# Attention with keys on partitions: row maxima ahead, probabilities stationary in the value product

## The chip, the cores and the metric

The kernel runs on one core of one Trainium2 chip. TensorE (PE in the profile; PEld is its weight load) multiplies matrices and accumulates in PSUM. It holds one operand, the weights or stationary side, loaded by an instruction of its own; the other operand, the moving side, then streams through it column by column. VectorE (DVE), ScalarE (ACT) and GpSimd (POOL) work on SBUF and PSUM, and SyncE (SP) issues transfers. Each engine has an instruction queue of its own that runs in order; semaphores hold an instruction until what it reads has been written. The metric is the device time of one execution in microseconds (us), the median over the runs.

## The reference

A sequence of 2048 tokens of width 1024 passes through a Mamba-2 layer, then through a latent attention layer with 16 heads, each with a residual addition; a last RMSNorm ends it. The change touches the attention of the second layer. A query and a key of a head have 96 entries (64 without and 32 with a rotary position), a value has 64.

```python
s = jnp.einsum('bqhd,bkhd->bhqk', q_nope[:, q0:kv_len], k_nope[:, :kv_len]) + \
    jnp.einsum('bqhr,bkr->bhqk', q_rope[:, q0:kv_len], k_rope[:, :kv_len])
s = s.astype(jnp.float32) * scale
mask = (q0 + local)[:, None] >= jnp.arange(kv_len)[None, :]
p = jax.nn.softmax(jnp.where(mask, s, -jnp.inf), axis=-1).astype(v.dtype)
outs.append(jnp.einsum('bhqk,bkhd->bqhd', p, v[:, :kv_len]))
...
o = o.reshape(Bsz, S, MLA_HEADS * V_HEAD) * jax.nn.silu(gate)
return o @ w_out
```

All of it is in fp32. The kernel keeps that precision with pairs of fp16 numbers, a high half and a low half (what the high one leaves); a product of two pairs is three matmuls, high by high, high by low and low by high.

## The kernel before

The program runs its stages one after the other on one core: the Mamba-2 layer, the projections of the attention layer, the attention itself (`attention`, `heads`), and `back`, which multiplies by the gate, projects, adds the residual and normalizes. The projections write K, V and Q as fp16 pairs to memory in the device (`kn_d`, `kr_d`, `v_d`, `qn_d`, `q1_d`, `q2_d`), and the attention loads them from there.

`heads` works through 64 jobs, 16 heads by 4 blocks of 512 queries. A job has units, one for each tile of 128 keys that its queries can see: 4, 8, 12 and 16 for the four blocks, 640 in all. The last four units of a job lie on the diagonal and are used for 512, 384, 256 and 128 queries.

The work of a job goes in two orders that are woven together:

- `scores` takes the four tiles of 128 queries (`j`) one by one. `cuts` divides the visible keys into chunks of at most 512. For each chunk `mm3` (L86 to L90) makes three matmuls with the queries stationary and the keys moving, into a PSUM bank "mm" (L1232; at the start also "tr"); the last chunk gets the causal mask by a further matmul (L1234). VectorE takes each chunk's row maximum (L1239) and, over the chunks, the negated one, `nm` (L1242, or L1237 where there is one chunk). ScalarE then takes the exponential with `nm` as bias and sums each row as it goes (L1247), a chunk at a time; the fp32 result `Pr` has queries on its partitions.
- `turn` makes the keys stand on partitions, unit by unit: up to four fp32 transposes on TensorE into a bank "tr" (L1272), a copy by ScalarE with a factor of 32768 for the high half of `PTs` (L1275), and the low half by VectorE, which reads the same bank (L1278).
- `values` multiplies, with the 128 columns of V (64 high, 64 low) stationary and the probabilities moving: one matmul for each half (L1292, L1293), accumulated over a job's units in another bank "tr".
- `finish` copies the outcome (L1299). SP stores 64 of its rows (L1301), and GpSimd's queue adds the other 64 to them in memory (L1305). The sums' reciprocals go to `ri_d` once a head (L1308 to L1317); `back` loads them, spreads each over 64 partitions and multiplies the gate by them (L1387, L1388).

The order of TensorE's instructions is the program's own (`manual_schedule`); the other engines' queues are set by a scheduler that follows it. The table `CREDIT` says, for each block, query tile and chunk, which turns ("T") and value products ("V") follow a chunk's scores; the first 20 chunks (`LAG`) have none behind them, and a value product comes at least two units (`DEPTH`) after its turn. So scores of one job stand among turns and products of the job before.

K, V and Q are loaded through GpSimd's queue (L1162 to L1176): K into a pool of two buffers, V and Q into "xT" buffers of which there are eight. Those of head h + 1 are ordered while head h is computed, K and V at its third block. SP's queue carries the stores, the weights and the loads of `back`.

Of the kernel before, what the change touches and what calls it, by code (L numbers as in the profile page):

```python
# [21 lines left out]
P = 128  # L22
# [5 lines left out]
NH = 16  # L28
# [9 lines left out]
NP = 24  # L38
# [3 lines left out]
LAG = 20  # L42
DEPTH = 2
CREDIT = (
    (("VT",), ("TV",), ("VT",), ("TV",)),
    (("", "VTVT"), ("", "TTVV"), ("", "TTVV"), ("", "TTVV")),
    (("TT", "", "VVTV"), ("TV", "", "VTTV"), ("TV", "", "TTVV"), ("TTV", "", "TVV")),
    (("T", "", "", "VVTTVTV"), ("T", "V", "", "VTTVTV"), ("T", "V", "V", "TVTTV"), ("TV", "V", "", "TVTVT")),
)
MAGIC = 12582912.0  # L50
PSCALE = 32768.0
# [20 lines left out]
class Net:  # L72
# [1019 lines left out]
    def mla_up(self, b, tables):  # L1092
# [24 lines left out]
        while ahead:  # L1117
            (n, w), ahead = ahead, next(todo, None)
            qT = self.qT
            for i in range(2 if n == 6 else 4):  # L1120
# [3 lines left out]
                elif n < 4:  # L1124
# [5 lines left out]
                    self.pair16(uv[:, :, 0, :], uv[:, :, 1, :], ps.rearrange("p (h d) -> p h d", h=8), 2.0 ** -15)  # L1130
# [10 lines left out]
    def open_heads(self):  # L1141

        self.tail = ExitStack()
        self.hp = self.tail.enter_context(
            self.tc.tile_pool(name="hp", bufs=2, side="right", reuse_waits="tile"))
        self.keys, self.vals, self.quer = {}, {}, {}
        self.load_k(0, 0, NB - 1)

    def load_vq(self):

        self.load_k(0, NB - 1, NB)
        self.load_q(0, 0)
        self.load_v(0)
        for n in range(1, NB):
            self.load_q(0, n)

    def load_k(self, h, lo, hi):

        nc, ts = self.nc, slice(lo * TB, hi * TB)
        if lo == 0:  # L1160
            self.keys[h] = self.t(self.hp, "K", [96, 2, T], F16, bufs=2)
        nc.gpsimd.dma_start(self.keys[h][0:64, :, ts], self.kn_d[h * 64:(h + 1) * 64, :, ts])  # L1162
        nc.gpsimd.dma_start(self.keys[h][64:96, :, ts], self.kr_d[:, :, ts])

    def load_v(self, h):

        V = self.vals[h] = self.t(self.xq, "xT", [P, T // P, P], F16, bufs=8)
        self.nc.gpsimd.dma_start(V, self.v_d[:, h * P:(h + 1) * P].rearrange("(k p) d -> p k d", p=P))

    def load_q(self, h, n):  # L1170

        nc, ts = self.nc, slice(n * TB, (n + 1) * TB)
        Q = self.quer[h, n] = self.t(self.xq, "xT", [96, 2, TB], F16, bufs=8)
        nc.gpsimd.dma_start(Q[0:64], self.qn_d[h * 64:(h + 1) * 64, :, ts])
        nc.gpsimd.dma_start(Q[64:80], self.q1_d[h * 16:(h + 1) * 16, :, ts])
        nc.gpsimd.dma_start(Q[80:96], self.q2_d[h * 16:(h + 1) * 16, :, ts])  # L1176
# [15 lines left out]
    def heads(self, sp):  # L1192
        nc, v = self.nc, self.nc.vector
        begun = []
        keys, vals, quer = self.keys, self.vals, self.quer

# [11 lines left out]
        def scores(h, qb, st):  # L1208

            if h + 1 < NH:  # L1210
                if qb == 2:
                    self.load_k(h + 1, 0, NB)
                    self.load_v(h + 1)
                self.load_q(h + 1, qb)
            Q, K = quer.pop((h, qb)), keys[h]
            late, total = [], sums[h][:, 4 * qb:4 * qb + 4]
            sm = self.t(sp, "sm", [P, 4, 4], bufs=2) if qb else total.unsqueeze(2)
            for j in range(4):
                qs = slice(j * P, (j + 1) * P)
                parts = cuts(qb * TB + (j + 1) * P)  # L1220
                nb = len(parts)
                mx, nm = (self.t(sp, m, [P, n], bufs=4) for m, n in (("mx", 4), ("nm", 1)))
                p = {}
                st["P"].append(p)
                banks = []
                for n, (c0, w) in enumerate(parts):
                    if late:
                        late.pop(0)()
                    begun.append(0)
                    s = self.t(self.pp, "tr" if len(begun) <= 18 and len(begun) % 2 == 1 else "mm", [P, TB], bufs=4)  # L1230
                    ks = slice(c0, c0 + w)
                    self.mm3(s[:, :w], Q[:, 0, qs], Q[:, 1, qs], K[:, 0, ks], K[:, 1, ks], True, n < nb - 1)  # L1232
                    if n == nb - 1:
                        nc.tensor.matmul(s[:, w - P:w], self.idb, self.mk, start=False, stop=True)  # L1234
                    banks.append((s, w))
                    if nb == 1:
                        v.tensor_reduce(nm, s[:, :w], AX.X, ALU.max, negate=True)  # L1237
                    else:
                        v.tensor_reduce(mx[:, n:n + 1], s[:, :w], AX.X, ALU.max)  # L1239
                    if n == nb - 1:  # L1240
                        if nb > 1:
                            self.last_max = v.tensor_reduce(nm, mx[:, :nb], AX.X, ALU.max, negate=True)  # L1242

                        def exp(n, j=j, nb=nb, parts=parts, banks=banks, nm=nm, p=p):
                            s, w = banks[n]
                            x = self.t(sp, "Pr", [P, TB], bufs=NP)
                            nc.scalar.activation(x[:, :w], s[:, :w], AF.Exp, bias=nm, accum_out=sm[:, j, n:n + 1])  # L1247
                            for c in range(0, w, P):
                                p[(parts[n][0] + c) // P] = x[:, c:c + P]
                            if j == 3 and n == nb - 1 and nb > 1:  # L1250
                                behind.append(lambda: v.tensor_reduce(total, sm[:, :, :nb], AX.X, ALU.add))
                                if nb != 3:
                                    behind.pop(0)()

                        late += [lambda n=n, f=exp: f(n) for n in range(nb)]
                        if nb > 2:
                            late.pop(0)()
                        if nb > 3 and j == 0:
                            with self.tc.issue_after(self.last_max.ins):
                                while behind:  # L1260
                                    behind.pop(0)()
                    self.place = qb, j, n, nb
                    yield CREDIT[qb][j][n]
            for f in late:
                f()

        def turn(h, qb, kb, st):

            jj = max(kb - 4 * qb, 0)
            pt = self.t(self.pp, "tr", [P, TB], bufs=4)  # L1270
            for j in range(jj, 4):
                nc.tensor.transpose(pt[:, j * P:(j + 1) * P], st["P"][j][kb], self.ident)  # L1272
            c = slice(jj * P, TB)
            u = self.t(sp, "PTs", [P, 2, TB], F16, bufs=5)
            nc.scalar.activation(u[:, 0, c], pt[:, c], AF.Copy, scale=PSCALE)  # L1275

            def low():
                v.scalar_tensor_tensor(u[:, 1, c], pt[:, c], PSCALE, u[:, 0, c], ALU.mult, ALU.subtract)  # L1278
# [269 lines left out]
```

## Time and profile before

| | |
|---|---|
| three runs | 3070.26, 3069.26, 3067.33 us; median 3069.26 us |
| profiled execution, its span | 3068.0 us |
| attention, from about 1998.5 to 2880.2 us | 881.7 us |
| behind it, `back` | 187.8 us |
| chain that ended last, by engine | PE 66%, DVE 16%, ACT 8%, issue 4%, DMA 4% |
| transfers in all | 457.10 MB, 149 GB/s in the mean |

The profile records one execution. A row of it gives a line of the kernel, the engine, the operation, the output and inputs by the program's names, and the shape; busy times are sums of records, which on TensorE overlap, since matmuls are pipelined. From the start of one matmul to the start of the next is what one takes of the array. "Idle before" is the time that an engine stood still ahead of a group's instructions, and behind it stands what ended it. "mm" and "tr" are PSUM banks, four each; "Pr" holds the exponentials, "PTs" the turned halves, "xT" is a buffer for several kinds of operand (V and Q here). A view of windows gives each engine's busy time and the granted clock of TensorE in a stretch.

### The profile page before, as it was taken

The page shows a single profiled execution, that of the slowest core. Times are in us where ns is not written, and L with a number is a line of the kernel's source. Part 1 is how long each engine was busy: PE and PEld are TensorE (multiplying, and loading weights), DVE is VectorE, ACT ScalarE, POOL GpSimd, SP SyncE. Part 2 cuts the span into 40 slices and gives each one's busy share as a digit, 9 for nine tenths or more (in the row PEclk, how much of TensorE's full clock was granted, in tenths as well). Part 3 has the DMA queues.
Part 4 walks back from the last instruction along what each step waited for, and adds up shares of the span by engine and source line. Part 5 has one row for each costly group of instructions (what it writes and reads, how often), then busy time and mean ns, then how long its engine had stood idle before and what let it go on. Part 6 is the DMA issues. An engine that isn't in the chain of part 4 may idle for free.

```text
span 3068.0 us, 51041 instructions
## 1 busy us (share of the span) xinstructions
PE 2988.2 (97%) x17758; PEld 1762.9 (57%) x17758; DVE 2309.3 (75%) x5034; ACT 1930.8 (63%) x4920; POOL 616.0 (20%) x842
## 2 busy tenths in 40 slices
PE   7899999999999999999999999999999999999998
PEld 3456655555555555545555455466666666666787
DVE  6789888778777787887755544488888888888576
ACT  8777656665666665565534333388888888888522
POOL 0212122211222122222111211322222222222100
PEclk9999999999999999999999999999999999999999
DMA  8665435454455466354466555622323223232484
GB/s 286 229 227 189 152 104 195 162 167 154 163 193 167 136 199 224 125 196 145 150 208 203 184 186 165 191 71 56 68 54 66 53 55 65 54 88 76 131 268 154
DMA packets 205065, 457.10 MB, mean 149 GB/s; under 512 B 28115, under 2 KB 57555, under 8 KB 203365
## 3 DMA queue, kind: packets, MB, share of 16 engines
q1 hardware_dynamic: 176948, 375.94, 38.0%
q0 software_dynamic: 27856, 77.89, 10.0%
q8 instruction: 140, 2.29, 0.3%
q14 instruction: 121, 0.98, 0.1%
HBM read 340.99 MB, written 112.73 MB: 148 GB/s over the span
## 4 chain that ended last, share of the span: by engine, by line
PE 66%; DVE 16%; ACT 8%; issue 4%; DMA 4%; SPq 1%; POOL 1%; ACTq 0%; DVEq 0%; POOLq 0%
PE mm L88 14%; PE mm L89 13%; PE mm L90 13%; PE tr L1272 6%; PE tr L89 4%; DVE cacc L616 4%; PE tr L88 4%; PE tr L90 3%; PE tr L1292 3%; PE tr L1293 3%; ACT Pr L1247 2%; PE tr L883 1%; ACT PTs L1275 1%; DMA big<-cumT 1%; DVE mx L1239 1%
## 5 line engine op out<-in xcount | busy, mean ns | idle before, releaser
L1278 DVE SCALAR_TENSOR_TENSOR PTs<-tr,PTs 128x512 f16<-128x512 f32 (+3 forms) x640 | 375.3, 607 | 103.0 <-ACT PTs L1275 95.1
L1247 ACT ACTIVATE Pr<-mm,nm 128x512 f32<-128x512 f32 (+2 forms) x631 | 398.0, 639 | 13.7 <-DVE nm L1242 13.5
L1275 ACT ACTIVATE PTs<-tr 128x512 f16<-128x512 f32 (+3 forms) x640 | 330.2, 542 | 119.9 <-PE tr L1272 111.0
L1239 DVE TENSOR_REDUCE mx<-mm 128x1 f32<-128x512 f32 (+2 forms) x569 | 335.1, 616 | 18.1 <-PE mm L90 15.2
L1272 PE MATMUL tr<-pack,Pr 128*128 128x128 f32 x2176 | 320.9, 273 | 6.5 <-DVE PTs L1278 2.4
L88 PE MATMUL mm<-xT,wsp 128*128 128x512 f16 x800 | 306.0, 383 | 7.1 <-ACT wsp L119 3.9
L89 PE MATMUL mm<-xT,wsp 128*128 128x512 f16 x800 | 305.2, 382 | 0.0
L90 PE MATMUL mm<-xT,wsp 128*128 128x512 f16 x800 | 304.7, 381 | 0.0
L1272 PEld LDWEIGHTS tr<-pack,Pr 128*128 128x128 f32 x2176 | 252.9, 141 | 80.1 <-ACT Os L1299 7.9
L88 PE MATMUL mm<-wsp,xT 128*128 128x512 f16 (+1 forms) x640 | 230.8, 362 | 4.8 <-ACT craw L610 4.7
L89 PE MATMUL mm<-wsp,xT 128*128 128x512 f16 (+1 forms) x640 | 231.9, 363 | 3.2 <-DVE wsp L120 3.2
L616 DVE SCALAR_TENSOR_TENSOR cacc<-craw,pack,cacc 128x512 f32<-128x512 f32 x288 | 215.6, 777 | 23.5 <-ACT cacc L614 22.5
L90 PE MATMUL mm<-wsp,xT 128*128 128x512 f16 (+1 forms) x640 | 231.9, 363 | 0.0
L88 PE MATMUL mm<-K,xT 96*128 96x512 f16 (+2 forms) x639 | 222.5, 348 | 5.3 <-ACT Pr L1247 3.3
L90 PE MATMUL mm<-K,xT 96*128 96x512 f16 (+2 forms) x639 | 221.8, 347 | 0.0
L1292 PE MATMUL tr<-PTs,xT 128*128 128x512 f16 (+3 forms) x640 | 221.0, 347 | 0.4 <-DVE PTs L1278 0.3
L89 PE MATMUL mm<-K,xT 96*128 96x512 f16 (+2 forms) x639 | 221.2, 346 | 0.0
L1293 PE MATMUL tr<-PTs,xT 128*128 128x512 f16 (+3 forms) x640 | 219.2, 347 | 0.0
L89 PEld LDWEIGHTS <-xT 128*128 128x128 f16 (+1 forms) x1408 | 137.9, 98 | 141.2 <-issue 30.9
L90 PEld LDWEIGHTS <-xT 128*128 128x128 f16 (+1 forms) x1408 | 136.8, 97 | 132.6 <-issue 4.8
L88 PEld LDWEIGHTS <-xT 128*128 128x128 f16 (+1 forms) x1408 | 137.4, 98 | 117.7 <-issue 4.7
L88 PE MATMUL mm<-wsp,yT 128*128 128x512 f16 (+1 forms) x512 | 197.5, 386 | 2.4 <-DVE sz L640 2.1
(458 smaller groups left out, 6801.3 us busy)
## 6 DMA issues: line engine op xcount, KB each, us to landing
wsp<-wi_d SPq DMA_DIRECT2D x96, 512.0 KB, 3.8
big<-cumT SPq DMA_DIRECT2D x64, 512.0 KB, 4.4
wraw<-in_ssm_w_out_dram SPq DMA_DIRECT2D x96, 256.0 KB, 3.6
wi_d<-wsp SPq DMA_DIRECT2D x32, 512.0 KB, 3.6
wsp<-wo_d SPq DMA_DIRECT2D x32, 512.0 KB, 3.5
wsp<-wu_d SPq DMA_DIRECT2D x28, 512.0 KB, 3.7
hx<-in_ssm_w_in_dram SPq DMA_DIRECT2D x48, 256.0 KB, 4.1
wraw<-in_ssm_w_in_dram SPq DMA_DIRECT2D x48, 256.0 KB, 3.9
```

Of the source, the lines that this page charges most:

```text
L88: mm(out, l_hi, r_hi, start=start, stop=False)
L89: mm(out, l_hi, r_lo, start=False, stop=False)
L90: mm(out, l_lo, r_hi, start=False, stop=stop)
L616: nc.vector.scalar_tensor_tensor(acc, raw[:, k:k + TB], wk[k], acc, ALU.mult, ALU.add)
L883: nc.tensor.matmul(yi[t, hc], E[:, h, t], Xd[:, hc], start=True, stop=True)
L1239: v.tensor_reduce(mx[:, n:n + 1], s[:, :w], AX.X, ALU.max)
L1247: nc.scalar.activation(x[:, :w], s[:, :w], AF.Exp, bias=nm, accum_out=sm[:, j, n:n + 1])
L1272: nc.tensor.transpose(pt[:, j * P:(j + 1) * P], st["P"][j][kb], self.ident)
L1275: nc.scalar.activation(u[:, 0, c], pt[:, c], AF.Copy, scale=PSCALE)
L1278: v.scalar_tensor_tensor(u[:, 1, c], pt[:, c], PSCALE, u[:, 0, c], ALU.mult, ALU.subtract)
L1292: nc.tensor.matmul(st["O"][:, c], vals[h][:, kb, :], u[:, 0], start=kb == 0, stop=False)
L1293: nc.tensor.matmul(st["O"][:, c], vals[h][:, kb, :], u[:, 1], start=False, stop=kb == nk - 1)
```

## The change

The maximum, the scores and the value product are each laid out anew, and the order table is replaced by rules.

**Maxima.** `maxima` makes only the high-by-high matmul of a chunk (L1235), masks the last chunk of a query tile (L1237), and takes the row maximum (L1238). At the end of a job the four maxima of each row become -max/64 + ln(16)/64, split into two fp16 halves in `turned` (L1243 to L1250). The maximum from the high halves need not be exact: the same number is taken out above and below the quotient. `row` turns these with one matmul (L1255), casts (L1257), stores them to `m_d` and loads them back (L1258, L1259, both on SP) into rows 96 and 97 of Q's high half, one query a column. Rows 96 and 97 of K's high half hold 64.0, so the subtraction becomes part of the score matmul.

**Scores.** A unit now has its keys stationary and up to 512 queries moving, so that the scores stand with keys on partitions at once (L1269 to L1271, three passes, the first with 98 rows). A diagonal unit gets the mask (L1273). ScalarE takes the exponential without bias or sums (L1275) into `x`, copies it from there as the high half (L1277), and the low half is `x` less the high half (L1279), on GpSimd for 128 of the units off the diagonal (two in five, by number) and on VectorE for 512.

**Value product.** The probabilities are stationary, for each 128 queries, and V moves: 130 columns for the high half (low V, high V, and two columns of 2^-14, by which the row sums come out), 66 for the low one (high V and those columns). `finish` adds the two parts, divides by the sum (L1306 to L1313), and `store` turns the outcome of two heads at once with four fp32 transposes (L1323), copies it (L1325) and stores 128 rows (L1327).

**Order.** At each unit come the maxima that are due (`due`: those of a job 7 units ahead, spread so that mostly one falls on a step), then rows or stores whose step has come (rows 2 steps after their last maximum, stores 4 steps after), then this unit's scores, then the value product of the unit 3 steps back (`HELD`). Ahead of the first unit stand 17 chunks of maxima.

**Loads and buffers.** K and V of a head lie in one of two fixed tiles, `K0` and `K1`. All loads of K, V and Q are on SP's queue: Q of a job when the maxima of the job two before it begin, K and V of head h + 2 behind the last value product of head h. `ri_d` and its loads and multiplication in `back` are gone.

```diff
@@ -1127,7 +1123,7 @@
-                    self.pair16(uv[:, :, 0, :], uv[:, :, 1, :], ps.rearrange("p (h d) -> p h d", h=8), 2.0 ** -15)
+                    self.pair16(uv[:, :, 1, :], uv[:, :, 0, :], ps.rearrange("p (h d) -> p h d", h=8), 2.0 ** -15)
...
-        nc.gpsimd.dma_start(Q[0:64], self.qn_d[h * 64:(h + 1) * 64, :, ts])
...
+        nc.sync.dma_start(Q[0:64], self.qn_d[h * 64:(h + 1) * 64, :, ts])
...
+        def maxima(n, j, i, c0, w, last):
...
+            mm(s[:, :w], Q[0:96, 0, qs], K[0:96, 0, c0:c0 + w], start=True, stop=not last)
+            if last:
+                mm(s[:, w - P:w], self.idb, self.mk, start=False, stop=True)
+            v.tensor_reduce(peak[n][:, j, i:i + 1], s[:, :w], AX.X, ALU.max)
...
+        def row(n):
+            ps = self.t(self.pp, "mm", [P, TB], bufs=4)
+            mm(ps[:, 0:P], turned[n % 2], self.idb, start=True, stop=True)
+            r = self.t(sp, "rT", [8, P], F16, bufs=2)
+            v.tensor_copy(r, ps[0:8, 0:P])
+            nc.sync.dma_start(self.m_d[n], r)
+            nc.sync.dma_start(quer[jobs[n]][96:98, 0, :], self.m_d[n].rearrange("(s j) q -> s (j q)", s=2))
...
+        def scores(i):
...
+            mm(s[:, c], K[0:98, 0, ks], Q[0:98, 0, c], start=True, stop=False)
+            mm(s[:, c], K[0:96, 0, ks], Q[0:96, 1, c], start=False, stop=False)
+            mm(s[:, c], K[0:96, 1, ks], Q[0:96, 0, c], start=False, stop=not diag)
+            if diag:
+                mm(s[:, jj * P:(jj + 1) * P], self.mk, self.idb, start=False, stop=True)
+            x = self.t(sp, "x", [P, TB], bufs=4)
+            act(x[:, c], s[:, c], AF.Exp)
+            u = self.t(sp, "PTs", [P, 2, TB], F16, bufs=HELD + 2)
+            act(u[:, 0, c], x[:, c], AF.Copy)
+            engine = nc.gpsimd if not diag and i % 5 in (1, 3) else v
+            engine.tensor_tensor(u[:, 1, c], x[:, c], u[:, 0, c], ALU.subtract)
...
+            for j in range(max(kb - 4 * qb, 0), 4):
+                o, js = outs[n][j // 2][:, j % 2], slice(j * P, (j + 1) * P)
+                mm(o[:, 0:130], u[:, 0, js], V[:, kb, :], start=kb == 0 and j % 2 == 0, stop=False,
+                   skip_group_check=True)
+                mm(o[:, 64:130], u[:, 1, js], V[:, kb, 64:130], start=False, stop=kb == 4 * qb + j,
+                   skip_group_check=True)
...
-                for j in range(2):
-                    nc.sync.dma_start(rb[j * 64:(j + 1) * 64], self.ri_d[2 * k + j, ts].partition_broadcast(64))
-                v.tensor_tensor(gt, gt, rb, ALU.mult)
```

What this moves on the engines shows in the order of their instructions. First TensorE in the middle of a head, before: the line, the operation, output and inputs, and the shape of the moving side; `Pr` are the exponentials of the four query tiles, `xT_25018` is Q and `K_24792` the keys.

```order
L1272 MATMUL tr_25802<-pack,Pr_25446 128x128
L1272 MATMUL tr_25802<-pack,Pr_25485 128x128
L1272 MATMUL tr_25802<-pack,Pr_25523 128x128
L1272 MATMUL tr_25802<-pack,Pr_25559 128x128
L88 LDWEIGHTS xT_25018
L88 MATMUL mm_25809<-K_24792,xT_25018 128x512
L89 LDWEIGHTS xT_25018
L89 MATMUL mm_25809<-K_24792,xT_25018 128x512
L90 LDWEIGHTS xT_25018
L90 MATMUL mm_25809<-K_24792,xT_25018 128x512
```

The same engine in such a place of the changed kernel: `xT_26832` is the Q of a coming job, `xT_26006` that of this one, `K_3813` and `K_3814` the tiles of two heads.

```order
L1235 LDWEIGHTS xT_26832
L1235 MATMUL mm_27247<-K_3813_20590,xT_26832 128x256
L1237 LDWEIGHTS idb
L1237 MATMUL mm_27247<-mk,idb 128x128
L1269 LDWEIGHTS K_3814_20591
L1269 MATMUL mm_27251<-xT_26006,K_3814_20591 128x512
L1270 LDWEIGHTS K_3814_20591
L1270 MATMUL mm_27251<-xT_26006,K_3814_20591 128x512
L1271 LDWEIGHTS K_3814_20591
L1271 MATMUL mm_27251<-xT_26006,K_3814_20591 128x512
L1291 LDWEIGHTS PTs_27196
L1291 MATMUL tr_27070<-K_3814_20591,PTs_27196 128x130
```

The transposes between scores and values are gone; a maximum's single pass stands in their place, and the weights of the value product are the probabilities, with a new load for each short matmul. The last two lines are one of eight such pairs of a full unit, four with 130 columns and four with 66.

ScalarE, ahead of the change, in the middle of a head:

```order
L1247 ACTIVATE Pr_24367,sm_24250<-mm_24332,nm_24329 128x512
L1275 ACTIVATE PTs_24389<-tr_24384 128x512
L1247 ACTIVATE Pr_24396,sm_24250<-mm_24346,nm_24329 128x512
L1247 ACTIVATE Pr_24411,sm_24250<-mm_24355,nm_24329 128x512
L1275 ACTIVATE PTs_24408<-tr_24403 128x512
```

And with it (`x` is the exponential in SBUF, `Ot` an output of the job before):

```order
L1275 ACTIVATE x_24862<-mm_24858 128x512
L1277 ACTIVATE PTs_24864<-x_24862 128x512
L1275 ACTIVATE x_24878<-mm_24874 128x512
L1306 ACTIVATE Ot_24885<-tr_24727 128x128
L1277 ACTIVATE PTs_24880<-x_24878 128x512
```

A copy now stands right behind the exponential whose outcome it reads, where before it read a transpose of an earlier exponential.

SP's queue in the changed kernel, at the end of a head (`K_3813` is refilled there for the head after the next, and `m_d` carries a job's maxima):

```order
L1162 DMA K_3813_20590<-kn_d 64x4096
L1163 DMA K_3813_20590<-kr_d 32x4096
L1168 DMA K_3813_20590<-v_d 128x16x128
L1258 DMA m_d<-rT_24627 8x128
L1174 DMA xT_25071<-qn_d 64x2x512
L1175 DMA xT_25071<-q_d 16x2x512
L1176 DMA xT_25071<-q_d 16x2x512
L1259 DMA xT_24035<-m_d 2x512
```

Before, this queue held only stores there (the outputs and, once a head, `ri_d`); the loads of K, V and Q stood on GpSimd's. A job's maxima now pass between those loads, store and load one after the other.

More of the change, by code (lines that the diff above doesn't have):

```diff
@@ L1206, in cuts @@
             return out
[L1208 to L1217, printed above, removed]
+        jobs = [(h, qb) for h in range(NH) for qb in range(NB)]
+        chunks, ends = [], []
@@ L1218, in scores @@
+        for n, (h, qb) in enumerate(jobs):
             for j in range(4):
-                qs = slice(j * P, (j + 1) * P)
                 parts = cuts(qb * TB + (j + 1) * P)
[L1221 to L1237, printed above, removed]
-                    else:
[L1239 to L1278, printed above, removed]
-            n, nb = self.place[2:]
-            if self.place[:3] == (NB - 1, 0, 0):
-                behind.append(low)
-            else:
-                with self.tc.issue_after(self.last_max.ins) if nb > 2 and n == nb - 1 else nullcontext():
-                    low()
-            return u[:, :, c], c
@@ L1319, in heads @@
-        jobs = [(h, qb) for h in range(NH) for qb in range(NB)]
-        states = [{"P": []} for _ in jobs]
-        sums = {}
-        def ahead():
-            for n, (h, qb) in enumerate(jobs):
-                if qb == 0:
-                    sums[h] = self.t(sp, "sum", [P, 16], bufs=3)
-                yield from scores(h, qb, states[n])
-        inverse, behind = [], []
-        units = [(h, qb, kb, states[n]) for n, (h, qb) in enumerate(jobs) for kb in range(4 * qb + 4)]
-        held = []
@@ new lines, in heads, with waiting @@
+        step, later, held, made = [0], [], [], 0
+        self.load_k(1, 0, NB)
+        self.load_v(1)
+        def waiting():
+            for at, f in list(later):
+                if at <= step[0]:
+                    later.remove((at, f))
+                    f()
+        for i in range(len(units)):
+            step[0] = i
+            while made < due[i]:
+                maxima(*chunks[made])
+                made += 1
+                n = chunks[made - 1][0]
+                if made == ends[n]:
+                    if i:
+                        later.append((i + ROWS, lambda n=n: row(n)))
+                    else:
+                        row(n)
+            waiting()
+            held.append((i, scores(i)))
+            if len(held) > HELD:
+                values(*held.pop(0))
@@ L1352, in back @@
+        while held:
+            step[0] += 1
+            values(*held.pop(0))
+            waiting()
+        while later:
+            step[0] += 1
+            waiting()
     def back(self):
```

178 lines of the change are left out of this document (103 added, 75 removed).

## The prediction

> **What bounds the kernel now.** I read the page first, for the span and the engines' busy time.
>
> ```profile
> span 3068.0 us, 51041 instructions
> ## 1 busy us (share of the span) xinstructions
> PE 2988.2 (97%) x17758; PEld 1762.9 (57%) x17758; DVE 2309.3 (75%) x5034; ACT 1930.8 (63%) x4920; POOL 616.0 (20%) x842
> ```
>
> The average says little, since the change lies in the attention stage and in the stage behind it. The view of windows gives those two by themselves (microseconds, then each engine's busy time, the granted clock and the DMA share).
>
> ```profile
> core 0: us, PE busy (x) PEld busy (x) DVE busy (x) ACT busy (x) POOL busy (x), PEclk, DMA share, GB/s
> 1998.50:2880.20 881.70, 869.42 (x5661) 567.00 (x5659) 746.00 (x1560) 729.24 (x2010) 199.31 (x289) 1.00 0.28 62
> 2880.20:3068.00 187.80, 177.38 (x759) 142.15 (x758) 115.97 (x230) 40.84 (x76) 0.82 (x1) 0.99 0.73 220
> ```
>
> The attention stage is 881.7 us, with TensorE busy for 869 of them at a granted clock of 1.00. VectorE (746) and ScalarE (729) stand at 85% and 83%: fewer TensorE columns bring a gain, but only down to those two.
>
> A busy TensorE isn't yet a full one, so I rebuild the stage from spacings, from start to start, in the timeline (start, duration, engine, line).
>
> ```profile
> 1998.83 0.22 PE L88 MATMUL tr<-K,xT 96*128 96x128 f16 x1
> 1998.89 0.22 PE L89 MATMUL tr<-K,xT 96*128 96x128 f16 x1
> 1998.94 0.22 PE L90 MATMUL tr<-K,xT 96*128 96x128 f16 x1
> 1999.00 0.22 PE L1234 MATMUL tr<-mk,idb 128*128 128x128 bf16 x1
> 1999.06 0.27 PE L88 MATMUL mm<-K,xT 96*128 96x256 f16 x1
> ...
> 2402.80 0.38 PE L1292 MATMUL tr<-PTs,xT 128*128 128x512 f16 x1
> 2403.02 0.38 PE L1293 MATMUL tr<-PTs,xT 128*128 128x512 f16 x1
> 2403.23 0.60 PE L1272 MATMUL tr<-pack,Pr 128*128 128x128 f32 x4
> ```
>
> A 512-wide matmul takes 0.215 us of the array (0.43 over two), a 128-wide one 0.056, and the mask product 0.06; widths between lie on that line (0.163 at 384, 0.109 at 256). Before each of the 128-wide ones here a new weight is loaded.
>
> ```profile
> L1272 PE MATMUL tr<-pack,Pr 128*128 128x128 f32 x2176 | 320.9, 273 | 6.5 <-DVE PTs L1278 2.4 <-ACT Os L1299 2.0
> L1247 ACT ACTIVATE Pr<-mm,nm 128x512 f32<-128x512 f32 x395 | 271.1, 694 | 13.7 <-DVE nm L1242 13.5
> L1239 DVE TENSOR_REDUCE mx<-mm 128x1 f32<-128x512 f32 x379 | 255.1, 684 | 17.7 <-PE mm L90 15.2
> L1278 DVE SCALAR_TENSOR_TENSOR PTs<-tr,PTs 128x512 f16<-128x512 f32 x448 | 299.5, 687 | 88.8 <-ACT PTs L1275 85.3
> L1275 ACT ACTIVATE PTs<-tr 128x512 f16<-128x512 f32 x448 | 257.4, 602 | 81.5 <-PE tr L1272 72.5 <-PE tr L1292 8.2
> L1278 DVE SCALAR_TENSOR_TENSOR PTs<-tr,PTs 128x128 f16<-128x128 f32 x64 | 18.3, 286 | 2.1 <-ACT PTs L1275 0.7
> ```
>
> These are groups by form: count, then busy time and mean ns, idle time before and its releasers. One fp32 transpose lasts 0.273 us and four in a row 0.60, so 0.11 each. The stage has 640 units (a block of 512 queries by 128 keys): 448 full ones, and 64 each of 384, 256 and 128 queries. One pass over all costs 448 x 0.215 + 64 x (0.163 + 0.109 + 0.056) = 117.3. So the stage's sum is 3 x 117.3 = 352 for scores, 256 x 0.06 = 15 for masks, 2176 x 0.11 = 239 for transposes and 2 x 117.3 = 235 for values: **841** of 881.7. The other 41 us are hand-offs.
>
> **The change, part by part.** *TensorE, removed:* 239 of transposes. *Added:* the maxima, one pass of high halves over the same columns, 117. Scores keep three passes, 352. Masks are now 512 (one per maximum tile, one per diagonal unit), 31. Rows, 64 x 0.06 = 4. Transposes ahead of the stores, 128 x 0.11 = 14.
>
> *The value product turns round:* the probabilities are the stationary side, 2176 blocks of 128 queries, each a 130-column matmul and a 66-column one, with a weight load for each (4352 where there were 1280).
>
> ```profile
> 612.55 1.15 PE L883 MATMUL tr<-Xd,big 128*64 128x64 f32 x32 [0.29 <-DVE pwx L148]
> ...
> 2401.35 0.10 PEld L1293 LDWEIGHTS <-xT 128*128 128x128 f16 x1
> 2401.35 0.22 PE L1292 MATMUL tr<-PTs,xT 128*128 128x128 f16 x1
> 2401.40 0.22 PE L1293 MATMUL tr<-PTs,xT 128*128 128x128 f16 x1
> ```
>
> The 130-column one is the 128-wide row, 0.056. No row shows 66 columns behind a load of 128. L883, of the first layer, has 64 columns behind loads of half the width, 32 in a row, at (1.15 - 0.22) / 31 = 0.030: the lower end. The 128-wide row, 0.056, is the upper one. I take 0.050, since with a full load a matmul starts 0.05 after its load began (2401.35 to 2401.40). So 2176 x 0.106 = 231, with ends of 187 and 244.
>
> Sum: 352 + 117 + 31 + 231 + 4 + 14 = **749**, from 705 to 762.
>
> *ScalarE.* The exponential reads PSUM as before, but without the row sums, whose read-out goes too; then a copy, from SBUF, makes the high half.
>
> ```profile
> 521.04 1.75 ACT L864 ACTIVATE Xw<-tr,d_wend 128x64 f32<-128x64 f32 x8 [0.39 <-DVE Xd L860]
> 522.63 0.36 ACT L868 ACTIVATE y<-tr,pack 128x64 f32<-128x64 f32 x1
> 522.83 0.69 ACT L805 ACTIVATE Xp<-Xw 128x512 fp32r<-128x512 f32 x1
> 523.36 0.67 ACT L618 ACTIVATE xs<-cacc 128x512 f32<-128x512 f32 x1
> ```
>
> L805 reads what L864 wrote and starts 0.04 after its end (521.04 + 1.75 = 522.79): a copy behind its own exponential waits for all of it. The next instruction follows an SBUF copy after 0.53. A PSUM pass of 512 lasts 0.60 (L1275), so a full unit is 0.60 + 0.04 + 0.53 = 1.17; each 128 queries fewer save 0.1 of both halves, so 0.97, 0.77 and 0.57. That is 448 x 1.17 + 64 x 2.31 = 672; with 128 output copies (0.18, estimated on the same slope) and 32 of 512 columns (0.48), **710**.
>
> *VectorE.* Its reductions stay: 117.3 / 0.215 full ones of 0.60 (record less the 0.08 by which neighbours overlap), 334 with the narrow ones. The subtraction now reads SBUF twice; 512 of 640 stay here at 0.60, 0.47, 0.34 and 0.20 (full to narrowest, the last from the 0.286 row), 257. Statistics, row casts and outputs, some 95. Sum **686**.
>
> *GpSimd* takes 128 of those subtractions.
>
> ```profile
> 612.42 0.68 DVE L834 TENSOR_TENSOR yt<-tr,d_ecum 128x512 f32<-128x512 f32 x1
> 612.43 1.28 POOL L806 TENSOR_TENSOR Xp<-Xw,Xp 128x512 fp32r<-128x512 f32 x1
> 613.02 1.24 DVE L619 SCALAR_TENSOR_TENSOR xs<-xs,cacc 128x512 f32<-128x512 f32 x1
> ```
>
> A GpSimd one lasts 1.28, and 128 of them 164 us: much room. But L619, with two SBUF operands, began beneath it and took 1.24; L834, with a PSUM operand, took 0.68. The moved subtraction has two SBUF operands, so VectorE may lose up to 0.55 per GpSimd unit: 0 to 70 us, which it has to spare in a stage of some 800. The unit itself has three full steps from its scores to its value product, each 0.645 for scores, 0.424 for values and 0.215 for a maximum: 3.84 us. It needs 0.38 (the last score matmul), 0.64 and 0.70 on ScalarE and 1.28 on GpSimd: 3.0. So I take 0.
>
> *Where the sum isn't TensorE's.* The engines' totals are close, so stretches differ. The first four steps of each head are narrow and carry maxima of full width: VectorE has about six reductions and four subtractions there, 5.5 us with the statistics, where TensorE has some 4.1: 1.4 more. In the next four ScalarE, at 1.17 a unit and with the output copies, has 5.3 where TensorE has 4.7: 0.6 more. 16 x 2.0 = 32. At the start, 17 maxima run ahead of the first unit: 17 x 0.60 = 10 on VectorE against 4 on TensorE, so 6. At the end no maxima are left and ScalarE sets the pace: 2. Together **41**, estimates from the durations above. Beside it I keep the old shortfall of **41**: the hand-offs are as many as before (640 units, 0.04 for each at least, 26), and the rows can be late.
>
> *The rows.* The maximum reaches the scores as two extra rows of Q: TensorE, a VectorE cast, a store and a load on SP's queue.
>
> ```profile
> K<-kn_d POOLq DMA_DIRECT2D x15, 512.0 KB, 5.0
> xT<-q_d POOLq DMA_DIRECT2D x128, 32.0 KB, 2.4
> ri_d<-rT SPq DMA_DIRECT2D x16, 8.0 KB, 1.8
> ```
>
> A small store lands after 1.8, a small load after 1.8 to 2.4: with 0.25 and 0.3 to 1.0 for the engines, 4.2 to 5.6. A query block with 16 units has its row ordered five steps, 5.5 us, ahead of its first score. The third block has nine, but in the new order its store stands right behind the next K and V on SP (5.0 for a half megabyte). What waits then is the score matmul, and with it all of TensorE. The 16 + 14 such rows cost 0 to 3 us each: 0 to 90; I take them as inside the 41.
>
> *Outside the stage.* K, V and Q loads move from GpSimd's queue to SP's, past the weights and the stores; 0, within 5 each way, as TensorE has 50 us of them ahead. The last stage loses its multiplication by the reciprocals.
>
> ```profile
> L1388 DVE TENSOR_TENSOR os<-os 128x512 f32<-128x512 f32 x30 | 20.7, 689 | 23.1 <-DMA os<-ri_d 23.1
> ```
>
> TensorE is busy for 177 of 188 there, so of 20.7 us of work and 23.1 of waiting at most 10 can be seen. I take 3.
>
> **Sum.** 749 + 41 + 41 = 831 for 881.7; 3068.0 - 881.7 + 831 - 3 = 3014. The runs' median, 3069.26, is 1.3 above the profiled execution's span: **3015**. The forecast's own range is 2985 (hand-offs hidden) to 3050 (the unknown ones at their upper ends).
>
> **Rivals.** *(a) Everything hides.* Narrow product at 0.030, no hand-offs: TensorE 705, ScalarE's 710 becomes the bound, with 60 for starts and late rows 770: 2953. For it: more units run ahead than before (17 chunks). Against it: 41 us were never hidden before.
>
> *(b) Weight loads set the pace, and the kernel is slower.* The load of 128 x 128 probabilities lasts 0.10 in its row. If 4352 loads stand one behind the other, the value product takes 4352 x 0.10 = 435 for 231, 204 more: 3219 at most. It turns the sign from 231 + 55 = 286, that is 0.066 a load, on. Against it: the rows above stand 0.05 to 0.06 apart with a load between each, though only for five in a row, and L883's 32 have half the load; for it: a full load lasts longer than either matmul. The Trainium skill, page "TensorE: Matmul & The Clock Gate", section "Back-to-back issue gap", speaks against the change here: a sustained stream of load and matmul pairs at 128 columns runs at about 81 ns a pair. By it the sum would be 4352 x 0.081 = 353, so 3137 as an estimate; this trace has 50 to 60 ns in short groups and can't show the sustained case.
>
> *(c) The low halves come late.* If each GpSimd subtraction is held up by one more of its length, 1.28, that is 0.44 past the slack of 0.84; for 128 units TensorE waits 56: 3071. L619 speaks for it, the spread of these units (two in five steps) against it.
>
> *(d) The rows come late.* Up to 30 x 3 = 90: 3105. This and (c) only decide if the order leaves no slack. That the change doesn't do what it says can be left out: the new order holds no probability transposes.
>
> **Chances.** Forecast 0.50, (a) 0.17, (b) 0.10, (c) 0.13, (d) 0.10. The range 2955 to 3090 leaves out (b), about half of (a) and a little of (d), some 0.2. About 0.2% (6 us) is what a measurement of this kernel can tell from no change. Faster: 0.50 + 0.17 + 0.07 of (c) + 0.04 of (d) = 0.78; same: 0.04 of (c) + 0.02 of (d) = 0.06; slower: 0.10 + 0.02 + 0.04 = 0.16.
>
> **What would show it.** The attention window should be near 831 with TensorE at 780 to 815 busy, and ScalarE and VectorE near 90%. Value matmuls of 130 and 66 columns should stand about 0.106 a pair; 0.13 or more is (b). Idle time of L1269 released by the row's load is (d); of L1293 released by GpSimd is (c), with VectorE's L1279 above 0.69. The last stage should be near 185. The forecast is wrong if ScalarE's exponential waits, or if hand-offs differ from 41 by more than half.

## The result, and the profile after

| | before | after |
|---|---|---|
| median of the runs | 3068.77 us (4 runs, 3067.33 to 3070.26) | 3012.67 us (4 runs, 3012.29 to 3013.76) |
| profiled execution, its span | 3068.0 us | 3010.9 us |
| ahead of the attention | 1998.5 us | 1995.6 us |
| attention, first maximum to last value product | 881.7 us | 827.5 us |
| behind it | 187.8 us | 187.8 us |

The kernel is faster, by 1.8%: the ratio is 0.9821, with a 95% interval from 0.9807 to 0.9835. The forecast was 3015.

The page's first lines, and below them the view of windows for the two stages of the kernel after:

```profile
span 3010.9 us, 55172 instructions
## 1 busy us (share of the span) xinstructions
PE 2871.6 (95%) x19726; PEld 1686.8 (56%) x19726; DVE 2281.5 (76%) x5162; ACT 1885.9 (63%) x4360; POOL 665.7 (22%) x798
```

```profile
core 0: us, PE busy (x) PEld busy (x) DVE busy (x) ACT busy (x) POOL busy (x), PEclk, DMA share, GB/s
1995.63:2823.10 827.47, 751.99 (x7616) 488.65 (x7615) 735.00 (x1715) 684.28 (x1447) 251.26 (x264) 0.97 0.22 54
2823.10:3010.90 187.80, 179.26 (x771) 144.01 (x770) 96.70 (x203) 42.81 (x78) 5.56 (x4) 0.99 0.52 178
```

Of the 57.1 us that the span lost, 54.2 are in the attention and 2.9 ahead of it; behind it nothing changed. The gain hides a surprise: TensorE's busy time fell by 117 us (869 to 752), far more than the stage did. TensorE now stands idle for 827.5 - 752.0 = 75.5 us where it stood for 12, and its clock is 0.97 of full speed in the mean where it was 1.00.

Two things above all were unlike the forecast. The first is the value product, in the timeline of TensorE (start, duration, engine, line):

```profile
2817.22 0.22 PE L1291 MATMUL tr<-K,PTs 128*128 128x130 f16 x1
2817.28 0.19 PE L1293 MATMUL tr<-K,PTs 128*128 128x66 f16 x1
2817.31 0.22 PE L1291 MATMUL tr<-K,PTs 128*128 128x130 f16 x1
...
2817.54 0.19 PE L1293 MATMUL tr<-K,PTs 128*128 128x66 f16 x1
2817.57 0.38 PE L1269 MATMUL mm<-xT,K 98*128 98x512 f16 x1
```

Four pairs take 0.35 us. Over the whole stage the mean from one 130-column matmul to the next within a unit is 0.0867 us (without the few that stand at half clock or behind a wait), so the narrow one costs 0.030 with its full load of 128 columns, and the product is 2176 x 0.0867 = 189 us, not 231.

The second is a new wait. The view of waits for TensorE (for whom, total, times, the longest), in the attention:

```profile
PE mm L1255 <- DVE nm L1250: 56.9, 49, 2.2
PE tr L1293 <- POOL PTs L1279: 6.2, 4, 2.1
PE mm L1255 <- DVE mx L1238: 3.8, 7, 0.5
PE mm L1269 <- DVE mx L1238: 3.4, 10, 0.6
```

L1255 is the matmul that turns a job's maxima into rows. It stands at a fixed place in TensorE's order, two steps behind the last maximum, and VectorE isn't done with the statistics by then. One such place, at the maxima of a third query block, first on TensorE:

```profile
2114.57 0.38 PE L1235 MATMUL mm<-K,xT 96*128 96x512 f16 x1
2117.03 0.23 PE L1255 MATMUL mm<-idb,nm 128*128 128x128 bf16 x1 [2.08 <-DVE nm L1250]
2117.10 0.22 PE L1269 MATMUL mm<-xT,K 98*128 98x128 f16 x1
...
2119.54 0.63 PE L1269 MATMUL mm<-xT,K 98*128 98x512 f16 x1
2119.97 0.63 PE L1270 MATMUL mm<-xT,K 96*128 96x512 f16 x1
2120.39 0.63 PE L1271 MATMUL mm<-xT,K 96*128 96x512 f16 x1
```

And on VectorE in the same stretch (the last maximum's matmul ended at 2113.31):

```profile
2112.71 1.34 DVE L1238 TENSOR_REDUCE mx<-mm 128x1 f32<-128x512 f32 x2
2114.13 0.69 DVE L1279 TENSOR_TENSOR PTs<-x,PTs 128x512 f16<-128x512 f32 x1
2114.74 0.16 DVE L1308 RECIPROCAL ri<-tr 128x2 f32<-128x2 f32 x1
2114.82 0.27 DVE L1310 TENSOR_TENSOR Oa<-tr,Ot 128x128 f32<-128x128 f32 x1
2115.01 0.15 DVE L1243 TENSOR_REDUCE m<-mx 128x4 f32<-128x12 f32 x1
2115.08 0.55 DVE L1279 TENSOR_TENSOR PTs<-x,PTs 128x384 f16<-128x384 f32 x1
2115.55 0.36 DVE L1247 TENSOR_SCALAR me<-m 128x4 f32<-128x4 f32 x1
2115.82 0.68 DVE L1238 TENSOR_REDUCE mx<-mm 128x1 f32<-128x512 f32 x1
2116.42 0.15 DVE L1249 CAST nm<-me 128x4 f16<-128x4 f32 x1
2116.49 0.41 DVE L1279 TENSOR_TENSOR PTs<-x,PTs 128x256 f16<-128x256 f32 x1
2116.83 0.15 DVE L1250 TENSOR_TENSOR nm<-me,nm 128x4 f16<-128x4 f32 x1
```

VectorE is never idle here. Four short statistics (L1243, L1247, L1249, L1250) have low halves, output work and the next maximum between them, and are done 3.7 us after the last maximum. TensorE waits 2.08. Then matmuls of 512 columns stand 0.43 apart instead of 0.215: the clock has gone to half, from 1.3 us behind the wait on and for 3.4 us. By blocks, the mean wait at L1255 is 0.82, 0.63, 2.05 and 0.33 us for first to fourth blocks, 61 us for the 64 jobs with the smaller releasers.

The trace's record of the granted clock has 13 stretches at half speed in the stage. One, of 10.2 us, lies at its start; the other 12 are of 3.4 us each, and 10 of them begin 0.2 to 1.6 us behind the wait of a third block. Half of their length is lost: 25.6 us in all, 5.1 of them at the start.

### The profile page after: what moved, and what is told of

It is laid out like the page before. It is cut to its first block, busy times and chain, and to the rows that moved or that the text cites. A ratio compares the mean times of both kernels' runs of the same rounds, so it can differ in the third digit from the quotient of the medians.

```text
span 3010.9 us, 55172 instructions
## 1 busy us (share of the span) xinstructions
PE 2871.6 (95%) x19726; PEld 1686.8 (56%) x19726; DVE 2281.5 (76%) x5162; ACT 1885.9 (63%) x4360; POOL 665.7 (22%) x798
## 4 chain that ended last, share of the span: by engine, by line
PE 60%; DVE 19%; ACT 10%; issue 6%; DMA 4%; POOL 1%; SPq 0%; ACTq 0%; DVEq 0%; POOLq 0%
PE mm L84 11%; PE mm L86 11%; PE mm L85 11%; PE tr L85 4%; PE tr L84 4%; PE tr L86 4%; DVE cacc L612 4%; ACT x L1275 3%; DVE PTs L1279 3%; DVE mx L1238 3%; ACT PTs L1277 2%; PE mm L1269 2%; PE mm L1270 2%; PE mm L1271 2%; PE tr L1291 2%
## 5 line engine op out<-in xcount | busy, mean ns | idle before, releaser
L1275 ACT ACTIVATE x<-mm 128x512 f32<-128x512 f32 (+3 forms) x640 | 336.1, 525 | 124.9 <-PE mm L1271 59.2
L1238 DVE TENSOR_REDUCE mx<-mm 128x1 f32<-128x512 f32 (+3 forms) x640 | 378.4, 602 | 39.3 <-PE mm L1237 23.4
L1277 ACT ACTIVATE PTs<-x 128x512 f16<-128x512 f32 (+3 forms) x640 | 361.7, 566 | 16.2
L1279 DVE TENSOR_TENSOR PTs<-x,PTs 128x512 f16<-128x512 f32 (+3 forms) x512 | 306.9, 604 | 45.3 <-ACT PTs L1277 35.2
L1291 PE MATMUL tr<-K,PTs 128*128 128x130 f16 x2176 | 280.0, 222 | 0.0
L1293 PE MATMUL tr<-K,PTs 128*128 128x66 f16 x2176 | 260.5, 194 | 9.0 <-POOL PTs L1279 6.2
L1291 PEld LDWEIGHTS <-PTs 128*128 128x128 f16 x2176 | 203.8, 98 | 61.4 <-issue 4.5
L1269 PE MATMUL mm<-xT,K 98*128 98x512 f16 (+3 forms) x640 | 227.2, 355 | 4.3 <-DVE mx L1238 3.4
L1293 PEld LDWEIGHTS <-PTs 128*128 128x128 f16 x2176 | 197.7, 98 | 59.7 <-POOL PTs L1279 7.9
L1270 PE MATMUL mm<-xT,K 96*128 96x512 f16 (+3 forms) x640 | 227.1, 355 | 0.0
L1235 PE MATMUL mm<-K,xT 96*128 96x512 f16 (+3 forms) x640 | 225.2, 358 | 1.1 <-DVE Xp L116 1.1
L1271 PE MATMUL mm<-xT,K 96*128 96x512 f16 (+3 forms) x640 | 225.6, 352 | 0.0
```

The lines of the kernel that those rows point to most:

```text
L1238: v.tensor_reduce(peak[n][:, j, i:i + 1], s[:, :w], AX.X, ALU.max)
L1269: mm(s[:, c], K[0:98, 0, ks], Q[0:98, 0, c], start=True, stop=False)
L1270: mm(s[:, c], K[0:96, 0, ks], Q[0:96, 1, c], start=False, stop=False)
L1275: act(x[:, c], s[:, c], AF.Exp)
L1277: act(u[:, 0, c], x[:, c], AF.Copy)
L1279: engine.tensor_tensor(u[:, 1, c], x[:, c], u[:, 0, c], ALU.subtract)
```

## The experiments

Each kernel is the one after with the edit shown; each ratio is to the kernel before, run on the same chip. By the ratio of 0.9821 the kernel after would take 3010 us there. In the edits, `READY` is the number of units by which the maxima run ahead, `ROWS` the number of steps from the last maximum to the row's matmul, and `HELD` the number from a unit's scores to its value product.

### e1_wide: what the value product's columns cost

```diff
-                mm(o[:, 64:130], u[:, 1, js], V[:, kb, 64:130], start=False, stop=kb == 4 * qb + j,
+                mm(o[:, 0:130], u[:, 1, js], V[:, kb, :], start=False, stop=kb == 4 * qb + j,
```

> The low half's value matmul is made 130 columns wide instead of 66 (low by low is added). In the trace of the change it costs 0.030 and a 130-column one 0.057, so TensorE gets 2176 x 0.027 = 59 us more. Theory A (the array's own sum sets the stage throughout, as the prediction's sum had it): 3012.7 + 59 = 3072. Theory B (in the narrow steps around each row VectorE is behind, and TensorE waits for it at the row's matmul, L1255): the columns added there fill the wait, the idle time of L1255 falls from 57 to 35 or less, and the kernel takes 3035 to 3055.

Measured: 3035.99 us, ratio 0.9904 (0.9887 to 0.9920). Its attention stage and TensorE's largest wait in it:

```profile
1995.47:2844.48 849.01, 792.49 (x7614) 538.79 (x7613) 747.48 (x1715) 702.03 (x1447) 240.59 (x264) 0.99 0.21 53
PE mm L1255 <- DVE nm L1250: 46.7, 36, 4.2
```

A pair now takes 0.113 in the mean, so 2176 x 0.0264 = 57 us were added to TensorE's sum, and the stage grew by 21.5 only (849.0). Some 33 of the rest can be found: TensorE's idle time fell from 75.5 to 56.5, and the clock lost 11.9 us instead of 25.6. L1255 waited 46.7 for VectorE instead of 56.9, where a fall to 35 or less was expected. So TensorE's sum isn't what sets the stage throughout. The run also sizes the forecast's error, as an estimate: had the pair cost 0.106, as forecast, the kernel would have come out near 3029 (3010 and 0.019 / 0.026 of the 26 us that this edit added).

### e2_rows4: the row's place in TensorE's order

```diff
-READY = 7
-ROWS = 2
+READY = 9
+ROWS = 4
```

> The row's matmul comes 4 steps behind the last maximum instead of 2, and the maxima 9 units ahead instead of 7, so that the row still has five steps to its first score. Theory B: L1255 waits only because it stands too early in TensorE's order; its 57 us of idle time go, with most of the clock dips behind them: 2940 to 2985. Rival: VectorE is the pace there whatever TensorE's order is, and the wait moves to the score banks (L1235 or L1269 released by L1238): 3000 to 3015.

Measured: 2970.77 us, ratio 0.9690 (0.9676 to 0.9705), 40 us below the kernel after by the ratios. Its waits and its attention stage:

```profile
PE mm L1269 <- ACT x L1275: 11.0, 27, 0.6
PE mm L1269 <- DVE mx L1238: 7.2, 15, 0.7
PE mm L1255 <- DVE nm L1250: 5.6, 10, 2.2
```

```profile
1993.09:2779.75 786.66, 745.08 (x7616) 487.67 (x7615) 728.69 (x1715) 685.21 (x1447) 234.07 (x264) 0.98 0.23 57
```

The wait at L1255 is gone but for 5.9 us of 61. Some of it came back elsewhere: L1269 waits 18 us for ScalarE and VectorE, where it waited 4, and TensorE's idle time fell by 34 us in all (75.5 to 41.6). The clock lost 11.9 us instead of 25.6: four stretches at half speed are left, one at the start and three in the last 110 us. Every engine has as many instructions as in the kernel after; only two numbers that set the order changed.

### e3_nopool: VectorE's share of the wait

```diff
-            engine = nc.gpsimd if not diag and i % 5 in (1, 3) else v
+            engine = v
```

> All low halves on VectorE, none on GpSimd: 128 x 0.60 = 77 us more on VectorE, 734 + 77 = 811 of a stage of 826. Theory B (VectorE's backlog is felt): the kernel takes 3040 to 3085, with more idle time at L1255. Rival (VectorE has room between the rows, only the row's place counts): 3008 to 3025. If GpSimd held VectorE up at the SBUF reads, VectorE's mean for a 512-wide L1279 falls from 708 ns towards 684.

Measured: 3090.57 us, ratio 1.0079 (1.0064 to 1.0094), slower than before the change, and 6 us above what theory B allowed. The stage and TensorE's largest wait in it:

```profile
1997.55:2903.74 906.19, 785.21 (x7616) 501.51 (x7615) 784.11 (x1843) 692.11 (x1447) 89.48 (x136) 0.94 0.20 50
PE mm L1255 <- DVE nm L1250: 106.0, 62, 3.6
```

The stage grew by 79 us: 49 more of idle time at L1255, and at a clock of 0.94 instead of 0.97 some 0.03 x 906 = 27 more. L1279 of 512 columns took 703 ns in the mean where it took 708, so GpSimd's reads cost VectorE almost nothing in that instruction on the average. VectorE's busy time grew by 49 us only (735.0 to 784.1) for some 77 of moved work; 20 of the difference are the statistics L1247, L1249 and L1250, which took 55.0 us beside GpSimd's work and 34.6 here (e9_apart comes back to that).

### e4_fill: where the clock dips come from

```diff
+            if jobs[n][1] == 2:
+                K, Q = keys[jobs[n][0] % 2], quer[jobs[n]]
+                for _ in range(9):
+                    mm(ps, K[0:96, 0, 0:P], Q[0:96, 0, :], start=True, stop=True)
             mm(ps[:, 0:P], turned[n % 2], self.idb, start=True, stop=True)
```

> Ahead of the row's matmul of each third query block stand 9 matmuls of 512 columns, 1.9 us, whose outcome is overwritten: they fill the 2.05 us wait for VectorE and compute nothing that is used. If the clock dips (matmuls of 512 columns at 0.43 instead of 0.215 some 1.3 us behind the wait, for about 3 us) come from the idle time, those after third blocks go, 1.0 to 1.7 us each, 16 of them: 2985 to 2998. If they have another cause: 3009 to 3016.

Measured: 3002.14 us, ratio 0.9794 (0.9780 to 0.9809), 8 us below the kernel after by the ratios, with intervals that just touch. The same place in its timeline (L1258 is the filling, L1259 the row's matmul), and its attention stage:

```profile
2116.59 0.38 PE L1235 MATMUL mm<-K,xT 96*128 96x512 f16 x1
2116.81 2.10 PE L1258 MATMUL mm<-xT,K 96*128 96x512 f16 x9
2119.06 0.23 PE L1259 MATMUL mm<-idb,nm 128*128 128x128 bf16 x1
```

```profile
1993.46:2811.06 817.60, 771.33 (x7760) 494.68 (x7759) 737.99 (x1715) 683.61 (x1447) 247.58 (x264) 0.99 0.22 55
```

The row's matmul comes as late as before, and 144 matmuls were added whose outcome is overwritten; yet the stage is 10 us shorter (827.5 to 817.6). Of the 13 stretches at half clock 2 are left, one of 20.5 us at the stage's start and one of 3.4. So the dips behind third blocks come from the idle time. Ten of them cost 17 us by the clock's record; the stage gained 10, as its start lost 5 more than before. I had expected 11 to 24 for 16 dips: only 10 of the 16 waits had been followed by one.

### e5_half and e10_rows4_nopool: VectorE, once the row is out of the way

Both have the rows of e2_rows4. In e5_half GpSimd takes 192 units, in e10_rows4_nopool none:

```diff
-READY = 7
-ROWS = 2
+READY = 9
+ROWS = 4
...
-            engine = nc.gpsimd if not diag and i % 5 in (1, 3) else v
+            engine = nc.gpsimd if not diag and i % 2 else v
```

```diff
-READY = 7
-ROWS = 2
+READY = 9
+ROWS = 4
...
-            engine = nc.gpsimd if not diag and i % 5 in (1, 3) else v
+            engine = v
```

> Rows at 4 steps and maxima 9 units ahead, as in e2_rows4 (2970.8), and GpSimd takes every second unit off the diagonal (192 instead of 128): 64 x 0.60 = 38 us less on VectorE, 64 x 1.17 = 75 more on GpSimd. If VectorE's backlog still costs in e2_rows4 (some 20 us of TensorE's idle time there name VectorE): 2950 to 2966. If what is left is TensorE's own work and ScalarE: 2967 to 2974. If GpSimd's 1.17 us come too late for the value product (rival c of the prediction), idle time of L1293 released by GpSimd grows past 15 us and the kernel takes over 2976.

Measured: 2972.98 us, ratio 0.9693 (0.9676 to 0.9709), the same as e2_rows4. L1293 waited 6.3 us for GpSimd, so rival (c) didn't come to pass with half as many again on GpSimd either.

> e2_rows4 with all low halves on VectorE. VectorE's 729 become about 806 of a stage of 787, so it sets the pace: stage 815 to 840, kernel 2996 to 3022 (25 to 50 over e2_rows4). If VectorE's work counts one for one whatever the row does, as the 81 us of e3_nopool suggest: 3045 to 3055.

Measured: 2992.91 us, ratio 0.9762 (0.9747 to 0.9776), just under the lower end of what was expected. The window of its attention:

```profile
1993.50:2806.00 812.50, 764.68 (x7623) 491.69 (x7621) 770.93 (x1844) 695.98 (x1449) 78.06 (x137) 0.98 0.23 56
```

The same 77 us of low halves on VectorE that cost 81 us with the row at two steps (e3_nopool) cost 22 with it at four, and VectorE's busy time grew about as much in both (49 and 42 us). Most of what GpSimd saved in the kernel after was thus the wait at the row and the clock behind it; less work for VectorE than it has in e2_rows4 brings nothing.

### e6_held4 and e8_rows6: more distance still

First e6_held4, then e8_rows6:

```diff
-HELD = 3
-READY = 7
-ROWS = 2
+HELD = 4
+READY = 9
+ROWS = 4
```

```diff
-READY = 7
-ROWS = 2
+READY = 11
+ROWS = 6
```

> e2_rows4 with the value product 4 units behind its scores instead of 3. If waits for the halves of the probabilities are still felt (L1293 idle for 8 us in e2_rows4): 2961 to 2967. If the units' hand-offs are hidden by now: 2968 to 2974.

> Rows 6 steps behind, maxima 11 units ahead. If the last 5.6 us of idle time at L1255 and what VectorE owes in the narrow steps can be spread further: 2958 to 2967. If the lead of 4 steps was enough: 2968 to 2975; if a longer start costs (more maxima ahead of the first unit): up to 2985.

Measured: 2974.52 us, ratio 0.9698 (0.9683 to 0.9714), and 2969.87 us, ratio 0.9685 (0.9671 to 0.9700). Neither can be told from e2_rows4. More distance for the value product brings nothing, and four steps are enough for the row.

### e7_late: the row without its lead

```diff
-ROWS = 2
+ROWS = 4
```

> Only the row's matmul moves to 4 steps behind the last maximum; the maxima stay 7 units ahead, so the row has 3 steps to its first score instead of 5 (for fourth blocks 5.25 us from the cast to the first score in the kernel after; some 2.7 here). Rival (d) of the prediction, by its price: if the store and the load need about 4 us, L1269 waits 1 to 2 us in each fourth block and less in others, 16 to 40 us with clock dips: 2985 to 3010. If they need under 2.7 us: as e2_rows4, 2968 to 2976.

Measured: 3028.16 us, ratio 0.9877 (0.9862 to 0.9892), slower than the kernel after and above what was expected.

```profile
PE mm L1269 <- DMA xT<-m_d: 38.2, 16, 3.6
```

L1255 waits only 4.4 us for its statistics now, but the 16 fourth blocks wait 2.4 us each for the row's load, and the clock in the stage falls to 0.95. From the cast's end to the first score pass 3.5 us there in the mean with the wait in it, where the kernel after has 5.25 and doesn't wait. So rival (d) is real, and lies some 1.7 us away from the kernel after. A later matmul alone isn't enough; an earlier maximum alone (`READY` 9 with `ROWS` 2) wasn't run.

### e9_apart: GpSimd kept away from the statistics

```diff
+        at, near = 0, set()
+        for i in range(len(units)):
+            while at < len(ends) and ends[at] <= due[i]:
+                near.update(range(i - 2, i + 3))
+                at += 1
+        free = [i for i, (n, kb) in enumerate(units) if kb < 4 * jobs[n][1] and i not in near]
+        away = {free[k * len(free) // 128] for k in range(128)}
...
-            engine = nc.gpsimd if not diag and i % 5 in (1, 3) else v
+            engine = nc.gpsimd if i in away else v
```

In the kernel after, one of the four statistics lasts strangely long. GpSimd and VectorE in the timeline, at the end of a second block:

```profile
2099.47 1.16 POOL L1279 TENSOR_TENSOR PTs<-x,PTs 128x512 f16<-128x512 f32 x1 [0.30 <-PE tr L1293]
2099.55 0.16 DVE L1243 TENSOR_REDUCE m<-mx 128x4 f32<-128x8 f32 x1
2099.74 0.91 DVE L1247 TENSOR_SCALAR me<-m 128x4 f32<-128x4 f32 x1
2100.68 0.17 DVE L1249 CAST nm<-me 128x4 f16<-128x4 f32 x1
```

L1247 works on four columns, and ends (2100.65) with GpSimd's instruction (2100.63). Counted by which records overlap, it took 0.675 us in the 45 jobs in which a GpSimd instruction ran beside it, and 0.162 in the other 19; in 43 of the 45 it ended 0.02 to 0.03 us behind that instruction.

> As the kernel after, with rows at 2 steps, but GpSimd's 128 low halves lie on units at least 3 steps away from the last maximum of a job. In the kernel after, the statistics instruction L1247 took 0.643 us in the 48 jobs in which GpSimd ran, to the end of GpSimd's instruction, and 0.160 in the 16 others. If GpSimd holds VectorE up there, L1247 of the second and fourth blocks falls to 0.16 to 0.37, and their waits at L1255 (0.63 and 0.33 us a job) fall by up to 0.3 each, more where the clock dips with them: 2995 to 3006 against 3009 to 3013. If VectorE's queue alone sets the row: 3008 to 3016.

Measured: 3033.33 us, ratio 0.9893 (0.9876 to 0.9910): slower than the kernel after, and above both ranges. L1247 (L1255 in this kernel) takes 0.160 us in second and fourth blocks and lies beside GpSimd in 15 third blocks only, so the hold is gone from the second and fourth. But the low halves that GpSimd no longer takes there stand in VectorE's queue, and the statistics of second blocks come 3.57 us after the last maximum instead of 2.75. In the view of waits (L1263 and L1258 are L1255 and L1250 of the kernel after):

```profile
PE mm L1263 <- DVE nm L1258: 75.6, 63, 2.3
```

VectorE's queue at the row is the larger cause. The hold's own share couldn't be tried by itself here, since every unit taken from GpSimd goes to VectorE; for the kernel after it stays open. With the row at four steps it matters little: in e2_rows4 L1247, L1249 and L1250 are held as well (62.3 us in all, where e3_nopool has 34.6), and L1255 waits only 5.9.

## Why the prediction was right, and where it was not

- **TensorE bound the stage, and the transposes' 239 us were worth a forecast of faster.** Right of the kernel before and of the sign. Scores and masks cost nearly what was forecast: 512 columns stand 0.215 to 0.220 apart, a mask's matmul takes 0.058. Of the kernel after it holds in part only: 57 us more for TensorE made the stage 21.5 longer (e1_wide). That the gain comes from the transposes rests on the sums (841 to 707) and on TensorE's busy time (869 to 752); no run changes them alone.
- **The value product, 231 us.** Too high by 42. The term that failed is the 0.050 for the narrow matmul: it was taken from a load's start to its matmul's start in a short group, which isn't a rate. L883's 0.030, with loads of half the width, was the better row, and it stood as the lower end. With it the sum is 352 + 117 + 31 + 189 + 4 + 14 = 707, not 749.
- **Hand-offs and uneven stretches, 41 + 41.** Too low by 38: the stage is 827.5 - 707 = 120 us above its sum, of which TensorE stands idle for 75.5 and the clock loses 25.6. By the prediction's own last sign, hand-offs that differ from 41 by more than half, its account of the waits was wrong: 120 less the 41 for uneven stretches is 79. The forecast had VectorE behind TensorE by 1.4 us in the narrow steps of each head, but saw no instruction that would wait for it at a fixed place. The row's chain was costed with 0.3 to 1.0 us for VectorE's cast behind the matmul, and nothing for its statistics ahead of it; those take 2.7 to 3.7. That wait is 61 us, and the clock loses some 20 outside the stage's start. With the row moved (e2_rows4) the stage is 786.7, 80 above its sum: about the 82 that the forecast had, though this doesn't show its two terms right. Of the 80, 41.6 are idle time and 11.9 the clock; what the rest is stays open.
- **VectorE, 686.** Too low by 49: it was busy for 735.0 us. L1247 alone took 33.4, where 64 times 0.162 would be 10. ScalarE, forecast at 710, was busy for 684.3.
- So 3015 was met by luck: two errors of some 40 us in the sum had opposite signs. The range didn't need the luck: with the first error alone, without the wait at the row, the kernel takes about 2971 (e2_rows4), with the second alone about 3029 (the estimate from e1_wide), and both lie inside 2955 to 3090.
- **Rival (b), weight loads set the pace.** Wrong. The 2176 pairs of a 130-column and a 66-column matmul, each behind its load, run at 0.0867 a pair, and in e1_wide, both of 130 columns, at 0.113, that is 0.0565 a matmul behind a full load. The 81 ns that the Trainium skill gives ("TensorE: Matmul & The Clock Gate", section "Back-to-back issue gap") for a sustained stream at 128 columns aren't seen here, and its 56 ns for an isolated one are. The pairs stand in groups of up to eight loads and matmuls between longer ones, so a stream longer than that isn't shown.
- **Rival (c), low halves late.** Wrong: 6.2 us, and 6.3 with 192 units (e5_half).
- **Rival (d), rows late.** Its price was right: e7_late shows 2.4 us for each fourth block. The kernel after escapes it, with 5.25 us where 3.5 don't do without a wait. What was late in it was not the transfer but the statistics ahead of it.
- **Queues and the last stage.** The loads on SP's queue cost nothing, as forecast: the part ahead of the attention is 2.9 us shorter, and its start varies from 1993 to 1998 us between the runs above. The 3 us of the last stage didn't come: 187.8 before and after. There 20.7 us of VectorE's work were removed that TensorE never waited for: in the kernel before, its only listed wait in that stage is one of 1.8 us, for ScalarE.

## What to carry to other kernels

Where one engine's order is written by hand, look at each instruction of it that reads another engine's short work, and count what is queued ahead of that work on the other engine; two numbers in the order were worth 40 us here, some 70% of what the whole change brought. A wait on TensorE can cost more than its length, since the clock may fall behind it (after 10 of 16 waits here). And when a forecast's sum comes out right, compare its terms before believing it.

## What the runs showed of the hardware

- A narrow matmul of 66 columns behind a full load of 128 x 128 takes 0.030 us, and one of 130 columns 0.057, 4352 in all, in groups of up to eight. By the 0.215 for 512 columns they would take 0.028 and 0.055, so the loads cost almost nothing that can be seen.
- An idle time of some 2.05 us can put TensorE at half speed: 10 of 16 such waits were followed, 0.2 to 1.6 us after the work resumed, by 3.4 us at half the clock. Filling that time with matmuls removed the dips there, and the stage was 10 us shorter (e4_fill). The Trainium skill ("TensorE: Matmul & The Clock Gate", section "HAM oscillation — how this bites in real kernels") speaks of idle gaps longer than about 3.4 us; here shorter ones were enough.
- A VectorE instruction on four columns of SBUF (L1247) took 0.675 us in the mean beside a GpSimd instruction and 0.162 without (45 and 19 jobs), and lasted to GpSimd's end. L1279, with two operands in SBUF, is held too where it begins well beneath one: in the kernel after, 27 of the 320 full ones began over 0.2 us ahead of a GpSimd instruction's end. All of these ended 0.55 us behind it and were 0.944 us long in the mean; the other 293 were 0.686. The Trainium skill ("SBUF — State Buffer", section "SBUF: two separate sides") describes a port pair that one of the two holds for a whole instruction, for VectorE with two SBUF inputs or in a two-port mode; the trace agrees for these L1279. L1247 is held to GpSimd's end as well; which mode it runs in, no run shows.
- Of the three engines said above to work on SBUF and PSUM, only VectorE and ScalarE touch a PSUM tile in the traces of the kernels before and after. GpSimd's instructions there lie in SBUF or issue transfers.

The longest of the held L1279 in the kernel after, and the GpSimd instruction above it:

```profile
2740.72 1.60 POOL L1279 TENSOR_TENSOR PTs<-x,PTs 128x512 f16<-128x512 f32 x1
2741.50 1.37 DVE L1279 TENSOR_TENSOR PTs<-x,PTs 128x512 f16<-128x512 f32 x1
```
